# A list scheduler that ranks by latest start in four passes, in a fused Fourier and DeltaNet layer

## The chip, the cores and the metric

The kernel runs on one core of a Trainium2 chip. The metric is the device time of one execution in microseconds (us), the median over runs. The core's engines are TensorE (PE, with its weight loads shown apart as PEld), VectorE (DVE), ScalarE (ACT), GpSimd (POOL) and SyncE (SP). SP and ACT also issue the transfers; the trace shows these issues as SPq and ACTq.

## The reference

One layer over 1024 latent tokens and 256 context tokens, 1024 channels wide. The input is normalised and modulated, and projected by `w_in` into all branches. A Fourier branch takes a 2-D transform in 4 channel groups. A DeltaNet branch has 8 heads of 128 channels, two directions and chunks of 64 tokens, and needs a triangular solve in each chunk. The two branches are merged through gates, projected by `w_out`, added to the residual and normalised.

```python
def deltanet_branch(qkv, dn_gate, ...):
    qkv = jax.nn.silu(centred_depthwise_conv(qkv, conv_w))      # 3 taps along the tokens
    ...
    a_mat = where(strict, einsum('bhnid,bhnjd->bhnij', kb, k) * decay, 0) + eye(CHUNK)
    sol = triangular_solve(a_mat, rhs, lower=True, unit_diagonal=True)
    ...                                                         # scan over the chunks, both directions
    return o @ w_dn_out, s_f, s_b

def merge_branches(r_f, r_d, y_f, y_d, w_out):
    return (sigmoid(r_f) * y_f + sigmoid(r_d) * y_d) @ w_out

x_next = layer_norm(DEEPNORM_ALPHA * x + gate_x * out_x) * ln_g + ln_b
```

## The kernel before

**Products.** Everything is float32. The large products are made of three matmuls each (`mm3`, L622 to L624) on operands that are split into a high and a low part: a cast on ACT gives the high part (L602, `whi`, `zh`, `h`), a subtraction on POOL or DVE the low part (L603, `wlo`, `zl`, `l`). A weight block of 128 x 1024 is loaded into one of two `wraw` buffers (L677), split, and used in 48 matmuls of 512 columns that fill one "main" PSUM bank of 1024. There are two main banks and four smaller "s" banks. PE can begin the next block when the block before the last one has been read out of its main bank.

**Stages.** First come the modulation and norms, the Fourier branch and the context's keys and values. Then, for each of the 8 heads: the q, k and v blocks with their convolution on DVE (L1002 and L1003 read the main bank `main` and write `cv`, ACT L1006 and POOL L1008 and L1009 finish them), the decays, the inverse, and the scan over ten units of 128 tokens. The inverse (L1182 to L1246) is turned on DVE (L1182), solved in 30 row steps there (L1193 and L1196), turned back (L1198, L1201), and then put together on PE from 32 x 32 blocks: 80 small matmuls L1216 into one PSUM tile, a copy (ACT L1217), 80 small matmuls L1223 into a second tile `y2`, of which DVE (L1226, L1227) and ACT (L1229) read 32 partitions at a time.

**Tail.** `tail()` (from L1536) multiplies the DeltaNet output by `w_dn_out` in 8 blocks `nb`. Blocks 0 and 1 are started early and hold the two main banks. `merged(nb)` ends a block: DVE L1549 multiplies the loaded token gate `td` with the bank, which sets the bank free, POOL L1550 adds the Fourier part `af`, and the sum is split into `zh` and `zl`. `td` and `af` come by SP (L1645, names `t<-td`, `t<-af`) into four buffers `t` of the pool `z`, which takes the place of the heads' pool `dn`. Then `gated(kt)` loads a block of `w_out` and multiplies it with the gate `gx` (L1565): blocks 2, 3, 6 and 7 (`RAW`) go through the two `wraw` buffers, the others through four buffers `wo`. `source(i)` loads a tile of x into `t`, and ACT issues the position rows (L1589). At the end come the last product and the norm (L1621 to L1641).

**The order.** The kernel is recorded first. `schedule()` then walks through planned time, keeps a free time for each engine, PSUM bank and the port that DVE and POOL share (`locked`), and always places next the operation that can begin earliest, by rank where several can. `ranks()` gives the rank: program order in the head and the tail, the length of the path to the end in between. `touch()` finds which operations depend on which. The real waits come from the framework that builds the program out of the resulting order.

## Time and profile before

| | before |
|---|---|
| median of 3 runs | 1348.24 us (1345.63 to 1352.89) |
| profiled execution | 1346.62 us |
| its span in the trace | 1344.8 us |
| PE, PEld busy | 94%, 77% |
| DVE, ACT, POOL busy | 67%, 43%, 31% |
| chain that ended last | PE 73%, DVE 14%, ACT 5%, DMA 4%, issue 3% |

The span is what lies between the first and the last record; 1.8 us of the execution lie around it. Busy shares are over the whole span, the granted TensorE clock is given per stretch (1.00 is the higher of its levels). The chain is followed back from the last instruction, at each step to what released it.

### The profile page before, as it was taken

The numbers are of one execution on the slowest core, as the hardware profiler recorded it, in microseconds if no ns is written. First come the engines' busy times: TensorE is split into PE (matmuls) and PEld (weight loads), VectorE is DVE, ScalarE is ACT, GpSimd is POOL, SyncE is SP. The second block draws the span as 40 slices with busy tenths as digits, with TensorE's granted clock in tenths as the row PEclk, the third lists the DMA queues.
The fourth block names the chain that finished last, engine by engine and source line by source line (L and its number), as shares of the span: only waits on it lengthen the run. The fifth ranks groups of instructions, "written<-read, shape, count | busy, mean of one in ns | idle before, by whom it ended". The sixth has DMA issues, their size and how long they took to land.

```text
span 1344.8 us, 22842 instructions
## 1 busy us (share of the span) xinstructions
PE 1263.5 (94%) x8274; PEld 1036.9 (77%) x8274; DVE 904.9 (67%) x2680; ACT 584.2 (43%) x1611; POOL 414.2 (31%) x390
## 2 busy tenths in 40 slices
PE   7899999999799999999999999899999999699797
PEld 1478888888678888888788888788877888588686
DVE  6867554306686977978767869657968545445597
ACT  2653333324455366474474474545464544212000
POOL 3532233134552323322223323223412013236210
PEclk9999999999999999999999999999988999799899
DMA  9524333352313103113022131132121025743332
GB/s 318 187 68 138 118 112 102 118 180 83 83 33 90 53 27 100 48 44 115 32 79 79 33 87 55 34 99 59 32 88 48 33 94 175 252 160 112 102 116 78
DMA packets 51893, 129.92 MB, mean 97 GB/s; under 512 B 6242, under 2 KB 18915, under 8 KB 51780
## 3 DMA queue, kind: packets, MB, share of 16 engines
q1 hardware_dynamic: 44496, 114.02, 26.9%
q10 hardware_dynamic: 7284, 14.45, 3.1%
q8 instruction: 65, 1.06, 0.3%
q14 instruction: 48, 0.39, 0.1%
HBM read 105.29 MB, written 23.15 MB: 96 GB/s over the span
## 4 chain that ended last, share of the span: by engine, by line
PE 73%; DVE 14%; ACT 5%; DMA 4%; issue 3%; POOL 0%; ACTq 0%; SPq 0%; DVEq 0%; POOLq 0%
PE main L622 17%; PE main L623 16%; PE main L624 16%; PE s L1281 2%; PE s L1139 2%; PE s L1298 2%; PE s L1268 2%; DVE B L1193 2%; PE s L1310 2%; DVE X L1196 2%; PE s L1277 2%; PE s L1037 2%; PE s L622 1%; PE s L624 1%; PE s L623 1%
## 5 line engine op out<-in xcount | busy, mean ns | idle before, releaser
L622 PE MATMUL main<-h,whi 128*128 128x512 f32 x1024 | 412.6, 412 | 21.2 <-DVE t L1549 12.2
L624 PE MATMUL main<-h,wlo 128*128 128x512 f32 x1024 | 413.4, 413 | 0.4 <-POOL wlo L603 0.4
L623 PE MATMUL main<-l,whi 128*128 128x512 f32 x1024 | 412.2, 411 | 0.0
L603 POOL TENSOR_TENSOR wlo<-wraw,whi 128x512 fp32r<-128x512 f32 (+1 forms) x136 | 185.8, 1373 | 514.1 <-ACT whi L602 399.5
L622 PEld LDWEIGHTS main<-h,whi 128*128 128x128 f32 x1024 | 194.8, 191 | 55.4 <-issue 13.8
L623 PEld LDWEIGHTS main<-l,whi 128*128 128x128 f32 x1024 | 194.8, 191 | 31.0 <-issue 0.2
L624 PEld LDWEIGHTS main<-h,wlo 128*128 128x128 f32 x1024 | 194.0, 191 | 30.4 <-POOL wlo L603 0.9
L602 ACT CAST whi<-wraw 128x512 fp32r<-128x512 f32 (+1 forms) x176 | 102.7, 600 | 181.6 <-PE main L623 114.1
L1284 ACT ACTIVATE y<-s,ce 128x128 f32<-128x128 f32 x144 | 52.7, 366 | 138.0 <-PE s L1281 137.1
L1156 POOL TENSOR_TENSOR E<-E,mask 128x256 f32<-128x256 f32 x80 | 58.3, 750 | 175.4 <-DMA E<-gr 136.8
L1193 DVE TENSOR_TENSOR B<-X 128x110 f32<-128x110 f32 (+27 forms) x472 | 103.3, 258 | 0.0
L1196 DVE TENSOR_TENSOR X<-X,B 128x110 f32<-128x110 f32 (+27 forms) x472 | 101.7, 256 | 0.0
L1143 DVE SCALAR_TENSOR_TENSOR zp<-s,c,E 128x256 f32<-128x256 f32 (+1 forms) x160 | 65.4, 452 | 45.1 <-PE s L1139 34.1
L1302 DVE SCALAR_TENSOR_TENSOR S<-S,egl,s 128x128 f32<-128x128 f32 x128 | 43.5, 342 | 50.9 <-PE s L1298 50.1
L1270 DVE SCALAR_TENSOR_TENSOR R<-s,eG,vt 128x128 f32<-128x128 f32 x144 | 49.7, 345 | 33.6 <-PE s L1268 31.8
L1160 ACT ACTIVATE E<-E,nG 128x128 f32<-128x128 f32 x160 | 53.8, 398 | 31.8 <-POOL E L1156 31.7
L603 DVE TENSOR_TENSOR wlo<-wraw,whi 128x512 fp32r<-128x512 f32 (+1 forms) x40 | 31.2, 781 | 51.7 <-ACT whi L602 51.7
L1281 PEld LDWEIGHTS s<-R,zp 128*128 128x128 f32 x288 | 52.1, 190 | 14.9 <-ACT zp L1286 2.8
L1281 PE MATMUL s<-R,zp 128*128 128x128 f32 x288 | 56.5, 278 | 3.2 <-ACT zp L1286 1.6
L1298 PE MATMUL s<-y,ktok 128*128 128x128 f32 x288 | 56.8, 280 | 2.4 <-DVE acc L1293 1.5
L1298 PEld LDWEIGHTS s<-y,ktok 128*128 128x128 f32 x288 | 49.9, 192 | 11.1 <-DVE acc L1293 1.9
L1268 PEld LDWEIGHTS s<-S,kq 128*128 128x128 f32 x256 | 45.8, 190 | 14.0 <-DVE S L1302 2.8
(340 smaller groups left out, 2424.3 us busy)
## 6 DMA issues: line engine op xcount, KB each, us to landing
wraw<-in_win SPq DMA_DIRECT2D x72, 512.0 KB, 3.7
E<-gr SPq DMA_DIRECT2D x40, 256.0 KB, 4.9
wmod<-in_wm SPq DMA_DIRECT2D x32, 256.0 KB, 5.9
x<-in_x SPq DMA_DIRECT2D x8, 512.0 KB, 5.8
wgate<-in_wg SPq DMA_DIRECT2D x8, 512.0 KB, 3.7
yf<-yf ACTq DMA_DIRECT2D x8, 512.0 KB, 2.7
rfy<-yf SPq DMA_DIRECT2D x8, 512.0 KB, 4.8
af<-rfy SPq DMA_DIRECT2D x8, 512.0 KB, 3.8
```

The source lines that it names most:

```text
L602: self.nc.scalar.copy(out=hi, in_=x)
L603: (eng or self.nc.gpsimd).tensor_tensor(out=lo, in0=x, in1=hi.bitcast(F32), op=ALU.subtract)
L622: mm(ps, lhsT=lh, rhs=rh, start=first, stop=False)
L623: mm(ps, lhsT=lh, rhs=rl, start=False, stop=False)
L624: mm(ps, lhsT=ll, rhs=rh, start=False, stop=last)
L1143: v.scalar_tensor_tensor(out=o, in0=ps.rearrange("p (a i) -> p a i", a=W), scalar=G.c[:, d, u:u + 1], in1=e[:, d, i].unsqueeze(1).to_broad ...
L1156: nc.gpsimd.tensor_tensor(out=e[:, d], in0=e[:, d], in1=self.mask[:, d].unsqueeze(1).to_broadcast([P, 2, P]), op=ALU.add)
L1193: v.tensor_tensor(out=B, in0=X[:, c0::2, l:l + 1].to_broadcast([P, w, l]), in1=X[:, l:l + 1, :l].to_broadcast([P, w, l]), op=ALU.mult)
L1196: v.tensor_tensor(out=X[:, c0::2, :l], in0=X[:, c0::2, :l], in1=B, op=ALU.subtract)
L1268: mm(ps, lhsT=G.k(u), rhs=S[d], start=True, stop=True)
L1281: mm(ps, lhsT=zp[:, d, u], rhs=R[d], start=True, stop=True)
L1298: mm(ps, lhsT=G.ktok[:, u], rhs=y[d], start=True, stop=True)
```

## The change

The instructions are nearly the same (6380 on PE in both); what differs is mainly their order and which buffers some tiles lie in.

1. `schedule()` runs four passes. Each pass (`place()`) is the old walk; after it `latest()` goes backwards through the order found and gives each operation the latest planned start that doesn't lengthen the plan. The next pass ranks by that, in the head and the tail too. The pass with the shortest plan is kept.
2. `touch()` counts a PSUM tile as a whole when it looks for dependencies.
3. The shared port is given back in the plan when the operation leaves its engine, not when its result has landed.
4. A new pool `share` holds three tiles of the inverse: X and Y (tag `s0`) and C (tag `s1`). In the tail the token tiles rotate over `s0`, `s1` and two buffers `t`. The first two, block 0's `td` and `af`, no longer wait for `dn` to close.
5. Blocks 6 and 7 of `w_out` are loaded into the buffers of `whi` and `wlo`.
6. The last tile's norm no longer gives half of its columns to ACT and POOL: L1628, L1630 and L1631 go, and L1636 runs on both halves.

```diff
...
-RAW = (2, 3, 6, 7)
+RAW = {2: 'wraw', 3: 'wraw', 6: 'whi', 7: 'wlo'}
...
+PASSES = 4
...
-        bits, (p0, p1) = v.bits, v.p
+        bits, (p0, p1) = v.bits, (0, P) if b.psum else v.p
...
     def schedule(self):
+
         self.finish()
         self.ranks()
+        best = None
+        for _ in range(PASSES):
+            done = self.place()
+            if best is None or self.span < best[0]:
+                best = self.span, done, {b: b.slot for o in done for b in o.opens or ()}
+            self.latest(done)
+        self.span, done, slots = best
+        for b, k in slots.items():
+            b.slot = k
+        return done
+
+    def latest(self, done):
+
+        end = self.span
+        after, late = dict.fromkeys(ENGINES, end), {}
+        for o in reversed(done):
+            l = min(end - (o.end - o.start), after[o.eng] - o.occ)
+            for s in o.succ:
+                k = s.pred[o]
+                l = min(l, late[s] - (o.occ if k == 1 else o.end - o.start + hop(o, s)))
+            for s in o.follow:
+                l = min(l, late[s])
+            late[o] = l
+            if o.eng == "PE":
+                after["PE"] = l
+        for o in done:
+            o.rank = -late[o]
+
+    def place(self):
...
             if o.lock:
-                locked["POOL" if e == "DVE" else "DVE"] = o.end
+                locked["POOL" if e == "DVE" else "DVE"] = t + o.occ + (1 if e == "DVE" and t != locked[e] else -30)
...
-        X = dn.tile([P, 32, 32], F32, tag="X", name="X")
+        X = self.share.tile([P, 32, 32], F32, tag="s0", name="X")
...
-            branches = lambda nb: (self._load(sp, "t", self.td[nb], 4), self._load(sp, "t", self.af[nb], 4))
+            turn = itertools.cycle((("s0", self.share, 1), ("s1", self.share, 1), ("t", sp, 2), ("t", sp, 2)))
+
+            def token(src):
+
+                tag, pool, bufs = next(turn)
+                return self._load(pool, tag, src, bufs)
+
+            branches = lambda nb: (token(self.td[nb]), token(self.af[nb]))
...
-                w = self._load(*((self.wp, "wraw", a["wo"][kt], 2) if kt in RAW else (sp, "wo", a["wo"][kt], 4)))
+                w = self._load(*((self.wp, RAW[kt], a["wo"][kt], 2) if kt in RAW else (sp, "wo", a["wo"][kt], 4)))
...
-                x = self._load(sp, "t", a["x"][i], 4)
+                x = token(a["x"][i])
...
-                if last:
-                    nm = sp.tile([P, 1], F32, name="nm")
-                    v.tensor_scalar(out=nm, in0=mv[:, 0:1], scalar1=-1.0, scalar2=None, op0=ALU.mult)
-                    c = halves[0]
-                    act.activation(out=y[:, c], in_=y[:, c], func=AF.Identity, bias=nm)
-                    gp.tensor_tensor(out=y[:, c], in0=y[:, c], in1=lng[:, c], op=ALU.mult)
...
-                for c in halves[last:]:
+                for c in halves:
...
-            self.C = self.dn.tile([P, 32, 32], F32, name="C")
+            self.C = self.share.tile([P, 32, 32], F32, tag="s1", name="C")
...
```

The lines of the changed kernel have other numbers: L1033 and L1034 are L1002 and L1003 of before, L1213, L1224 and L1227 are L1182, L1193 and L1196, L1229 and L1232 are L1198 and L1201, L1254 is L1223, L1372 is L1341, L1587 is L1549, L633 and L634 are L602 and L603.

**The entry of the tail, DVE.** The rows begin with the last gate products of head 7 (`silu`); `wlo` are low parts of the weights of blocks 2 and 3. Before:

```order
L1341 SCALAR_TENSOR_TENSOR silu_11863<-s,cst,silu_11863 128x512 x2
L603 TENSOR_TENSOR l_12014<-silu_11863,h_12009 128x512
L603 TENSOR_TENSOR wlo<-wraw,whi 128x512 x2
L1549 SCALAR_TENSOR_TENSOR t<-t,main 128x1024 x2
L603 TENSOR_TENSOR zl_12116<-t,zh_12106 128x1024
```

Now, with `s_11405` the tile of block 0 in the pool `share`:

```order
L1372 SCALAR_TENSOR_TENSOR silu_11867<-s,cst,silu_11867 128x512 x2
L634 TENSOR_TENSOR l_12018<-silu_11867,h_12013 128x512
L1587 SCALAR_TENSOR_TENSOR s_11405<-s_11405,main 128x1024
L634 TENSOR_TENSOR wlo<-wraw,whi 128x512
L1587 SCALAR_TENSOR_TENSOR t<-t,main 128x1024
L634 TENSOR_TENSOR wlo<-wraw,whi 128x512
```

Block 0's L1587 stands ahead of both `wlo`, block 1's between them.

**The entry of the tail, ACT,** with the semaphores that each waits for (those that begin with DMAHW are of transfers). Before:

```order
L1560 DMA gx<-gx 128x1024 [waits DMAHW0_49,DVE_49,DMAHW7_49,PE_49,Pool_49]
L1577 DMA lng<-in_lng 128x1024
L1578 DMA lnb<-in_lnb 128x1024
L1580 DMA ec<-in_ec 128x512
L602 CAST whi<-wraw 128x512 [waits DMAHW0_49,PE_49]
L602 CAST whi<-wraw 128x512
L1589 DMA rows<-in_er 64x512 [waits DMAHW0_49]
L1589 DMA rows<-in_er 64x512 [waits DMAHW1_49]
L1589 DMA rows<-in_er 64x512 [waits DMAHW3_49]
L1589 DMA rows<-in_er 64x512 [waits DMAHW4_49]
L602 CAST whi<-wraw 128x512 [waits DMAHW6_49,PE_49]
```

Now:

```order
L1598 DMA gx<-gx 128x1024 [waits DMAHW1_49,DVE_49,DMAHW2_49,PE_49,Pool_49]
L1627 DMA rows<-in_er 64x512 x3
L633 CAST whi<-wraw 128x512 [waits DMAHW2_49,PE_49]
L633 CAST whi<-wraw 128x512
L1627 DMA rows<-in_er 64x512 [waits DMAHW1_49]
L1618 DMA ec<-in_ec 128x512 [waits DMAHW2_49]
L1616 DMA lnb<-in_lnb 128x1024 [waits DMAHW4_49]
L1615 DMA lng<-in_lng 128x1024 [waits DMAHW6_49]
L633 CAST whi<-wraw 128x512 [waits DMAHW0_49,PE_49]
```

Four issues that wait for earlier transfers stand ahead of block 3's `whi` in both; they are other ones.

**The 32 x 32 products of the last head's inverse, PE,** with waits. Before:

```order
L1310 MATMUL s<-zp 128x128 [waits Activation_49]
L1223 MATMUL s<-C,Y 32x32 [waits DVE_49]
L1223 MATMUL s<-Ct,Y 32x32
...
L1223 MATMUL s<-C,Y 32x32
L1223 MATMUL s<-Ct,Y 32x32 [waits Activation_49]
L1223 MATMUL s<-C,Y 32x32
```

Now:

```order
L1308 MATMUL s<-S_10542,kq 128x128 [waits Activation_49]
L1254 MATMUL s<-C,Y 32x32 [waits DVE_49]
L1254 MATMUL s<-C,Y 32x32
L1254 MATMUL s<-Ct,Y 32x32 x2
...
L1254 MATMUL s<-Ct,Y 32x32 x2
L1299 MATMUL s<-S_10546,kq 128x128 [waits DVE_49]
```

The second wait, in the middle of the run, is gone. Before, seven of the eight inverses have it; now none does.

**The first head's inverse, DVE,** from the turn of C into X on; `cv<-main` are the convolutions that read a main bank, 511 and 512 columns each. Before:

```order
L1182 STREAM_TRANSPOSE X<-C 128x1024
L1002 SCALAR_TENSOR_TENSOR cv<-main,cst,cv 128x511
L1002 SCALAR_TENSOR_TENSOR cv<-main,cst,cv 128x512
L1193 TENSOR_TENSOR B<-X 128x30
...
L1193 TENSOR_TENSOR B<-X 128x126
L1003 SCALAR_TENSOR_TENSOR cv<-main,cst,cv 128x512
L1003 SCALAR_TENSOR_TENSOR cv<-main,cst,cv 128x511
L1002 SCALAR_TENSOR_TENSOR cv<-main,cst,cv 128x511
L1002 SCALAR_TENSOR_TENSOR cv<-main,cst,cv 128x512
L1003 SCALAR_TENSOR_TENSOR cv<-main,cst,cv 128x512
L1003 SCALAR_TENSOR_TENSOR cv<-main,cst,cv 128x511
```

Now:

```order
L1213 STREAM_TRANSPOSE X<-C 128x1024
L1033 SCALAR_TENSOR_TENSOR cv<-main,cst,cv 128x511
L1033 SCALAR_TENSOR_TENSOR cv<-main,cst,cv 128x512
L1034 SCALAR_TENSOR_TENSOR cv<-main,cst,cv 128x512
L1034 SCALAR_TENSOR_TENSOR cv<-main,cst,cv 128x511
L1224 TENSOR_TENSOR B<-X 128x30
...
L1229 STREAM_TRANSPOSE C<-X 128x32x32
L1033 SCALAR_TENSOR_TENSOR cv<-main,cst,cv 128x511
L1232 STREAM_TRANSPOSE Ct<-C 128x640
L1033 SCALAR_TENSOR_TENSOR cv<-main,cst,cv 128x512
L1034 SCALAR_TENSOR_TENSOR cv<-main,cst,cv 128x512
L1034 SCALAR_TENSOR_TENSOR cv<-main,cst,cv 128x511
```

The first block's convolution is now done before the row steps, the second block's after them; before, both ended in the middle.

## Rows read from the trace of the kernel before

**Rows 1.** page, part 1: busy us, share of the span, instructions
```profile
PE 1263.5 (94%) x8274; PEld 1036.9 (77%) x8274; DVE 904.9 (67%) x2680; ACT 584.2 (43%) x1611; POOL 414.2 (31%) x390
```

**Rows 2.** windows: stretch, length, busy us (x) of PE PEld DVE ACT POOL, PEclk, DMA share, GB/s
```profile
0.00:350.00 350.00, 328.14 (x1670) 252.98 (x1671) 187.27 (x376) 140.35 (x289) 120.30 (x135) 1.00 0.42 139
350.00:408.00 58.00, 47.74 (x428) 38.05 (x427) 50.41 (x176) 28.16 (x75) 30.28 (x20) 0.91 0.21 56
408.00:1100.00 692.00, 672.74 (x5181) 567.40 (x5181) 521.73 (x1849) 368.43 (x1151) 193.03 (x192) 0.99 0.21 64
...
1157.00:1170.00 13.00, 0.85 (x3) 0.50 (x2) 4.14 (x4) 1.14 (x2) 2.31 (x3) 0.64 1.02 358
...
1245.00:1256.00 11.00, 3.60 (x10) 2.07 (x9) 9.21 (x9) 3.32 (x5) 3.83 (x4) 0.70 0.70 206
```

**Rows 3.** waits of PE, whole span: engine line <- releaser: us, times, longest
```profile
PE main L622 <- DVE t L1549: 12.2, 1, 12.2
PE main L622 <- ACT kq L1006: 8.1, 1, 8.1
PE main L622 <- ACT h L602: 7.0, 1, 7.0
...
PE s L1223 <- ACT zp L1229: 4.6, 4, 2.5
...
PE s L1223 <- DVE T L1226: 1.9, 3, 0.7
```

**Rows 4.** timeline 1150 to 1172: start, us, engine, line, operation [idle before <- releaser]
```profile
1152.01 1.22 DVE L603 TENSOR_TENSOR l<-silu,h 128x512 fp32r<-128x512 f32 x1 [0.69 <-ACT h L602]
...
1153.35 0.32 SPq L1645 DMA_DIRECT2D t<-td  x1
...
1157.93 7.63 ACTq L1589 DMA_DIRECT2D rows<-in_er  x4
...
1165.66 1.14 ACT L602 CAST whi<-wraw 128x512 fp32r<-128x512 f32 x2 [9.08 <-DMA t<-af]
...
1166.88 1.33 DVE L603 TENSOR_TENSOR wlo<-wraw,whi 128x512 fp32r<-128x512 f32 x1 [8.86 <-ACT whi L602]
1168.14 2.34 DVE L1549 SCALAR_TENSOR_TENSOR t<-t,main 128x1024 f32<-128x1024 f32 x2
```

**Rows 5.** chain that ended last, 1165 to 1180: start, us, what
```profile
1173.68 0.43 PE main L622
...
1174.52 0.23 PE main L624
```

**Rows 6.** DMA issues, 1150 to 1172: KB each, median us to landing
```profile
t<-td SPq DMA_DIRECT2D x3, 512.0 KB, 5.8
```

**Rows 7.** timeline 1242 to 1257
```profile
1242.62 2.02 SPq L1645 DMA_DIRECT2D wraw<-in_wo  x2
...
1250.57 2.35 DVE L1565 TENSOR_TENSOR wraw<-wraw,gx 128x1024 f32<-128x1024 f32 x2
1251.88 2.28 ACT L602 CAST h<-wraw 128x512 fp32r<-128x512 f32 x4 [2.48 <-DMA rows<-in_er]
...
1252.55 1.22 PE L622 MATMUL main<-h,zh 128*128 128x512 f32 x2 [7.05 <-ACT h L602]
```

**Rows 8.** timeline of DVE, 352 to 392
```profile
368.24 1.40 DVE L1003 SCALAR_TENSOR_TENSOR cv<-main,cst,cv 128x512 f32<-128x512 f32 x2
...
386.46 2.06 DVE L1198 STREAM_TRANSPOSE C<-X 128x1024 f32<-128x1024 f32 x1
```

**Rows 9.** timeline 1336 to 1345
```profile
1336.46 0.74 DVE L1636 SCALAR_TENSOR_TENSOR yr<-yr,mv,lng 128x512 f32<-128x512 f32 x1
...
1337.44 1.26 POOL L1631 TENSOR_TENSOR yr<-yr,lng 128x512 f32<-128x512 f32 x1 [31.31 <-ACT yr L1630]
1337.49 1.23 DVE L595 TENSOR_TENSOR fint<-finy 128x1 f32<-128x1 f32 x1
...
1339.14 0.16 DVE L595 TENSOR_TENSOR fint<-finy 128x1 f32<-128x1 f32 x1
```

More of the change, by code (lines that the diff above doesn't have):

```diff
@@ L1211, in inverse @@
         y1, y2 = self.s()[:, :32 * NU], self.s()[:, :32 * NU]
-        Y = dn.tile([P, 32, 32], F32, tag="X", name="Y")[:, :NU]
+        Y = self.share.tile([P, 32, 32], F32, tag="s0", name="Y")[:, :NU]
         pairs = ((0, 0, 1), (0, 2, 3), (1, 1, 0), (1, 3, 2))
@@ L1233, in inverse @@
             y1, y2 = self.s()[:, :64 * n], self.s()[:, :64 * n]
-            Y = dn.tile([P, 32, 32], F32, tag="X", name="Y")[:, :16].rearrange("p (u a) i -> p u (a i)", a=2)[:, :n]
+            Y = self.share.tile([P, 32, 32], F32, tag="s0", name="Y")[:, :16].rearrange("p (u a) i -> p u (a i)", a=2)[:, :n]
             for u in us:
@@ L1678, in run @@
             self.both = False
+        self.share = self.pool("share")
         with ExitStack() as es:
```

## The prediction

> **What bounds the kernel now.** I read the page's busy shares first: PE is busy for 94% of the span and PEld for 77%, the next engine, DVE, for 67% [rows 1]. PE is the bound, its instructions stay the same, and so an order can only give back the time in which PE stands still or runs at its lower clock. The second view is the table of stretches, which shows where that is [rows 2]. Up to 350 us PE stands for 350 - 328.1 = 21.9 us; from 350 to 408 us for 10.3 us; from 408 to 1100 us, through seven heads, for only 692 - 672.7 = 19.3 us; from 1157 to 1170 us for 12.15 us, nearly the whole stretch; from 1245 to 1256 us for 7.4 us. The third view is the list of PE's waits, which names the releasers [rows 3]: the three longest single waits are 12.2 us for L1549 (the entry of the tail), 8.1 us for L1006 (the first head's inverse) and 7.0 us for a high part `h` (the last product). Then there is a wait of 4.6 + 1.9 us in seven pieces before L1223. These four places are what I cost; the rest of the order I treat as one term.
>
> **Entry of the tail.** The reader follows one timeline [rows 4]. The pool `dn` closes with the DVE subtraction that begins at 1152.01 us and takes 1.22 us; only then, at 1153.35 us, SP can issue the first `t<-td`. On ACT four issues of `rows` stretch over 7.63 us from 1157.93 us on, although each such issue is short: they wait, one by one, for earlier transfers. Behind them stands the cast of block 3's `whi` at 1165.66 us, behind that on DVE its `wlo` at 1166.88 us, and behind that, in DVE's order, L1549 at 1168.14 us, which alone could have set the main bank free for block 2. So PE waits for a block that it doesn't need yet. In the new order block 0's L1587 stands ahead of both `wlo`, and its tile lies in `share` and was loaded well before `dn` closed. It needs only block 0's last matmul, which PE reaches some 15 matmuls before its work is used up; 15 x 0.23 us = 3.4 us [rows 5] against 1.2 us for L1587 (2.34 us for two, [rows 4]). Block 2 can then begin without a wait.
>
> What is late next is block 3. PE works 48 matmuls x 0.23 us = 11 us on block 2, from about 1157.4 to 1168.4 us. By then block 1's bank must be free (its `td` is issued first after the close; such a load landed in 5.8 us in the median [rows 6], so about 1160 us) and block 3's `whi` and `wlo` must be done. If ACT's cast ends as before, at 1165.66 + 1.14 = 1166.8 us, and DVE's subtraction at 1168.2 us, it just fits. Price: 12.15 us of idle time, and the matmuls after it, which run at the lower level of the clock: in the chain they are 0.43 us each up to 1173.68 us and 0.23 us from 1174.52 us on [rows 5], the stretch's mean granted clock is 0.64 [rows 2]. Twelve of them cost 12 x 0.20 = 2.4 us. I leave 1 us for what remains: 12.15 + 2.4 - 1.0 = **-13.5 us** (from -8.5, with 6 us left for block 3, to -14.5).
>
> **The last product.** `w_out` blocks 6 and 7 went through the `wraw` buffers; the two issues are at 1242.62 us, their multiplication L1565 at 1250.57 us, the cast at 1251.88 us, and PE goes on at 1252.55 us after 7.05 us [rows 7]. In the new order they go into buffers of `whi` and `wlo`, which come free as blocks 6 and 7 of the DeltaNet product use theirs up; SP issues them ahead of the x tiles, and DVE has multiplied both before the last L1587. Price: 7.4 us idle [rows 2], and ten matmuls that took 3.60 us instead of 10 x 0.23 = 2.3 us at a mean clock of 0.70, 1.3 us more. I leave 2 us, as `zh` of block 7 still stands behind an issue of `rows` on ACT: 7.4 + 1.3 - 2.0 = **-6.7 us** (from -4.7 to -8.7).
>
> **The 32 x 32 products.** Before, the plan took the four quadrants of the tile `y2` as independent, and the real waits are on the whole tile: PE stopped in the middle of L1223's run until a reader of the finished quadrants was done. Now all 80 come first and the readers after. Price: the 4.6 + 1.9 = **-6.5 us** of [rows 3]. Against it the readers begin later, at most by half a run in eight heads; I take the near end and keep 3.5 us as the far one.
>
> **The first head's inverse.** Before, PE waited 8.1 us, since the convolution that frees a main bank ran only at 368.24 us, in the middle of the row steps [rows 3, 8]. Now it runs before them, so this wait goes. But the second block's convolution stands behind the whole inverse, after the turn back, which began at 386.46 us before [rows 8]. PE has 48 matmuls, 11 us, for the 25 us from 361.5 us to there. Before, after the wait it had both blocks and worked on until the inverse was through. I count it thus: the new order has some 25 matmuls (5.7 us) less behind it when the small products begin, and they begin about 2.7 us earlier, as two of four convolution pairs no longer lie within the row steps (1.40 us for a pair [rows 8]). Net **+3 us** (from -5, if other work fills the hole, to +6).
>
> **The end.** L1636 costs 0.74 us once more. It takes the place of L1630 and L1631, beside which DVE's L595 took 1.23 us where the same operation takes 0.16 us [rows 9]; this 1.07 us and the small L1628 go: **-0.5 us** (from 0 to -0.6).
>
> **The rest of the order.** In seven heads 19.3 - 6.5 = 12.8 us of PE's idle time are left [rows 2, 3], in many small waits of the scan. I take a quarter of it, **-3 us**; it can't be more than -12.8, and a poorer order could add as much as half, +6. Up to 350 us only few places move; I take nothing, and a fifth of the 21.9 us, 4 us, to either side. The passes themselves cost nothing on the chip, since they run when the program is built.
>
> Sum: -13.5 - 6.7 - 6.5 + 3 - 0.5 - 3 = -27.2 us on the profiled 1346.62 us, which gives 1319.4 us; the median of the runs shown is 1.6 us above the profiled execution, which is less than the terms are sure to. **Forecast: 1319 us.**
>
> **Rivals.**
> *B, the wait at the tail's entry only moves.* For it speaks that the transfers were saturated there: 358 GB/s over 13 us, the engines' share 1.02 [rows 2], 4.7 MB; only two loads of 0.5 MB leave this stretch, and in the new order four ACT issues that wait for earlier transfers still stand ahead of block 3's `whi`. Against it speaks that these wait for transfers that were issued early, and that block 3 now has 11 us of cover. If `whi` comes 9 us later than before, PE waits that long after block 2, the term falls from -13.5 to -4.5, and the time is 1328; with 3 us more left at the last product 1331. I give it 1325 to 1338. The Trainium skill, "DMA: Bandwidth & Descriptors", section "Issuing engines are not separate DMA queues", says that transfers from different issuing engines run on the same 16 engines and interleave, so that another order of issues doesn't shorten a burst; by this alone the burst would last as long less the two loads moved out of it, and this rival is what follows. The trace agrees in that SP's and ACT's issues land slowly together.
>
> *C, slower: banks held behind the inverse in every head.* What the first head shows could happen in all: a convolution put off behind the row steps. From 368.24 to 386.46 us are 18.2 us [rows 8]; less the 11 us that PE has in the other bank, a head could lose 7.2 us. Seven heads undo the gain from 27.2 / 7 = 3.9 us a head on, and at 5.5 us the time is 1319 + 38.5 = 1358. Against it: in the other heads PE also has the previous head's scan, and in the new order their convolutions stand within the row steps.
>
> *D, more than forecast.* If half of the 12.8 us goes (3.4 us more), the first inverse gains 5 us instead of losing 3, and the first 350 us give 4, the time is 1319 - 15 = 1304.
>
> *E, nothing that can be told.* If the heads' order costs 6 us instead of giving 3, half of the tail's 20 us comes back in another place and L1223 gives 3.5 us, it is 1319 + 9 + 10 + 3 + the 3 us of the worst first inverse = 1344.
>
> **How the numbers follow.** The forecast (1308 to 1327) gets 0.60, B 0.18, D 0.10, C 0.06, E 0.06. Half a per cent, 6.7 us, is about what a measurement of this kernel can tell from no change (the three runs shown lie 0.5% apart), so faster is below 1341.5. A, B and D lie there, less a little of B's upper end: 0.87; same 0.07; slower 0.06. The range goes from 1305 to 1338: it holds the forecast, B and half of D, 0.83, and leaves out C, E and D's lower half.
>
> **What would show it.** In the changed kernel's list of waits, PE's wait for the bank at the tail's entry should be under 2 us, and block 2's matmuls should run 0.23 us apart from the first; a wait of 6 us or more some 11 us later is B. The stretch before the last product should have no wait over 2 us. L1254 should have no idle time before it but at the start of a run. Around 373 to 388 us there should be a wait of some 10 us or more on a main bank, in place of the one at 361.5 us. If waits of over 3 us on main banks appear in each head, C holds. What would make the forecast wrong most easily is the seven heads: nearly all their instructions stand in another order, and I price that by one quarter of a small idle time.

## The result and the profile after

| | before | changed |
|---|---|---|
| median | 1350.36 us (1345.63 to 1352.89, 4 runs) | 1314.14 us (1308.25 to 1315.54, 4 runs) |
| profiled execution | 1346.62 us | 1308.25 us |
| span in the trace | 1344.8 us | 1306.5 us |

The ratio is 0.9727 [0.9685 to 0.977], faster by 36 us in the median. The profiled execution of the changed kernel is the fastest of its four, 6 us below their median (mean granted clock 0.985, in the others 0.982 to 0.983), so sums made from its trace lie at the fast edge.

The page, part 1, of the changed kernel (the columns of [rows 1]):

```profile
PE 1252.5 (96%) x8274; PEld 1027.8 (79%) x8274; DVE 921.2 (71%) x2680; ACT 586.5 (45%) x1610; POOL 415.4 (32%) x389
```

PE did the same work (8274 matmul records in both traces; the 6380 given above counts PE's instructions in the program) in 1252.5 us instead of 1263.5 us [rows 1], and stood for 1306.5 - 1252.5 = 54.0 us instead of 1344.8 - 1263.5 = 81.3 us. So the 38.3 us by which the span is shorter are 27.3 us of standing and 11.0 us in which the same work ran faster. I had looked almost only for the first kind. A part of the 11.0 us may belong to this execution and its clock, not to the order; 5.7 us of it are found below, in the 640 small products.

The stretches of the changed kernel that answer to [rows 2], with the same columns. Its later parts lie earlier in time: 1140 to 1160 us holds the entry of the tail, 1210 to 1230 us the last product.

```profile
0.00:350.00 350.00, 330.02 (x1656) 253.52 (x1657) 184.73 (x375) 139.69 (x285) 121.83 (x133) 0.98 0.43 139
350.00:408.00 58.00, 46.12 (x385) 37.31 (x384) 50.88 (x170) 25.38 (x69) 26.31 (x21) 0.85 0.23 65
408.00:1080.00 672.00, 659.41 (x5179) 554.45 (x5178) 530.93 (x1840) 368.78 (x1139) 192.35 (x194) 1.00 0.23 66
...
1140.00:1160.00 20.00, 20.00 (x90) 16.57 (x89) 11.01 (x8) 4.53 (x7) 8.17 (x4) 1.00 0.95 347
...
1210.00:1230.00 20.00, 20.00 (x89) 16.43 (x88) 19.97 (x14) 2.19 (x3) 17.37 (x10) 1.00 0.20 66
```

In both stretches of the tail PE is busy for the whole 20.00 us at the higher level of the clock (granted 1.00); before, 12.15 us and 7.4 us of idle time stood there [rows 2]. The first inverse (350 to 408 us) stands for 11.9 us, 1.6 us more than before. The heads (408 to 1080 us) stand for 12.6 us; before, it was 19.3 us.

The list of PE's waits that answers to [rows 3]:

```profile
PE s L1068 <- DVE kq L1042: 8.6, 2, 7.3
PE main L877 <- DVE cs L814: 5.2, 1, 5.2
PE s L1312 <- DVE acc L1324: 3.6, 2, 3.1
PE s L1247 <- DVE Ct L1232: 2.7, 1, 2.7
...
PE main L653 <- ACT h L633: 1.3, 1, 1.3
```

All four places that were costed have left the head of the list. What leads it now is the first head's inverse in a new form (L1068, L1247), and no wait on a main bank in any head (L653 to L655) is longer than 1.3 us, so rival C did not occur.

**The entry of the tail.** First SP's issue of block 0's later tile (its `af` was issued at 1057.27 us), then ACT and DVE there, by the timeline of each engine (columns as in [rows 4]):

```profile
1070.24 0.32 SPq L1677 DMA_DIRECT2D s<-td  x1
```

```profile
1151.05 0.33 ACTq L1615 DMA_DIRECT2D lng<-in_lng  x1
1151.48 1.14 ACT L633 CAST whi<-wraw 128x512 fp32r<-128x512 f32 x2 [8.04 <-DMA wo<-in_wo]
```

```profile
1141.32 1.22 DVE L1587 SCALAR_TENSOR_TENSOR s<-s,main 128x1024 f32<-128x1024 f32 x1 [1.46 <-PE main L655]
1143.54 1.36 DVE L634 TENSOR_TENSOR wlo<-wraw,whi 128x512 fp32r<-128x512 f32 x1 [1.00 <-ACT whi L633]
1144.82 1.21 DVE L1587 SCALAR_TENSOR_TENSOR t<-t,main 128x1024 f32<-128x1024 f32 x1
1152.66 1.41 DVE L634 TENSOR_TENSOR wlo<-wraw,whi 128x512 fp32r<-128x512 f32 x1 [6.64 <-ACT whi L633]
```

Block 0's tiles were issued 71 us and more before DVE uses them. DVE's L1587 for block 0 begins 1.46 us after DVE came free, released by PE's last matmul; this is the wait that should remain, on DVE's side and not on PE's. Block 3's `whi` is still late: it stands behind issues on ACT that wait for transfers, and begins at 1151.48 us. It sets off DVE's `wlo`, which is done at 1154.1 us. PE is still busy with block 2 then and wants it only about 1155.5 us (an estimate: 48 matmuls, 10.9 us, before PE's last matmul of block 3, which sets off that block's L1587 at 1166.48 us). So the end of the burst that rival B speaks of is hidden behind block 2, with about 1.5 us to spare.

The burst itself is there as before: in the 32 us from about the close of the pool `dn` on, the transfers ran at 299 GB/s and a share of 0.82 (1139 to 1171 us), before at 304 GB/s and 0.84 (1153 to 1185 us). The Trainium skill, "DMA: Bandwidth & Descriptors", section "Issuing engines are not separate DMA queues", says that transfers issued by different engines run on the same 16 DMA engines and interleave; the trace agrees in that the other order of issues left these two figures as they were. What changed is what waits for the burst.

**The last product.** DVE's timeline:

```profile
1202.37 1.59 DVE L1603 TENSOR_TENSOR whi<-whi,gx 128x1024 f32<-128x1024 f32 x1 [2.03 <-DMA whi<-in_wo]
...
1206.12 2.32 DVE L1603 TENSOR_TENSOR wlo<-wlo,gx 128x1024 f32<-128x1024 f32 x1
...
1210.00 1.22 DVE L1587 SCALAR_TENSOR_TENSOR t<-t,main 128x1024 f32<-128x1024 f32 x1 [1.56 <-PE main L655]
```

As forecast, both multiplications lie ahead of the last L1587, and the wait of 7.0 us is gone.

**The small products.** All of L1223 before, and all of L1254 after, by windows of one line (columns: PE busy, PEld busy, PEclk, DMA share, GB/s):

```profile
0.00:1345.00 1345.00, 12.78 (x640) 11.09 (x640) 0.98 0.30 97
```

```profile
0.00:1306.00 1306.00, 7.09 (x640) 6.20 (x640) 0.99 0.31 99
```

Not only the idle time before these 640 matmuls went (6.5 us to 0.1 us); the matmuls themselves take 7.09 us instead of 12.78 us.

**The first inverse.** PE's timeline:

```profile
375.32 0.25 PE L1118 MATMUL s<-part,fold 128*32 128x8 f32 x8
382.85 1.11 PE L1068 MATMUL s<-cst,kq 128*128 128x128 f32 x4 [7.28 <-DVE kq L1042]
385.32 1.12 PE L1068 MATMUL s<-cst,kq 128*128 128x128 f32 x4 [1.35 <-DVE kq L1042]
...
389.55 0.27 PE L1247 MATMUL s<-Ct,zp 32*32 32x32 f32 x2 [2.68 <-DVE Ct L1232]
```

A hole of some 10 us was forecast between 373 and 388 us. It is there, 7.28 + 1.35 + 2.68 = 11.3 us. The instruction that stands first is L1068, which waits for DVE's `kq` (L1042, at 382.12 us among the row steps) and which PE's order puts ahead of the next main bank's matmuls; a wait on a bank was forecast.

**The end.** DVE's timeline:

```profile
1298.71 0.74 DVE L1668 SCALAR_TENSOR_TENSOR yr<-yr,mv,lng 128x512 f32<-128x512 f32 x1
...
1300.28 0.16 DVE L626 TENSOR_TENSOR fint<-finy 128x1 f32<-128x1 f32 x1
...
1302.03 1.54 DVE L1671 SCALAR_TENSOR_TENSOR yr<-yr,finy,lnb 128x512 f32<-128x512 f32 x3
```

From L1668 to L1671 it takes 1302.03 - 1298.71 = 3.3 us; before, it was 3.9 us, from 1336.46 us [rows 9] to L1639 at 1340.38 us. The small operation beside POOL's L1631 took 1.23 us [rows 9] and now, with POOL idle, 0.16 us.

### The profile page after: what moved, and what is told of

It is laid out like the page before. It is cut to its first block, busy times and chain, and to the rows that moved or that the text cites. A ratio compares the mean times of both kernels' runs of the same rounds, so it can differ in the third digit from the quotient of the medians.

```text
span 1306.5 us, 22833 instructions
## 1 busy us (share of the span) xinstructions
PE 1252.5 (96%) x8274; PEld 1027.8 (79%) x8274; DVE 921.2 (71%) x2680; ACT 586.5 (45%) x1610; POOL 415.4 (32%) x389
## 4 chain that ended last, share of the span: by engine, by line
PE 55%; DVE 5%; ACT 2%; issue 1%; DMA 1%; DVEq 0%; ACTq 0%; SPq 0%
PE main L653 12%; PE main L654 12%; PE main L655 12%; PE s L1312 2%; PE s L1329 2%; PE s L1299 2%; PE s L1170 2%; PE s L1308 2%; PE s L1068 1%; PE s L1341 1%; DVE B L1224 1%; PE s L654 1%; PE s L655 1%; PE s L653 1%; DVE X L1227 1%
## 5 line engine op out<-in xcount | busy, mean ns | idle before, releaser
L653 PE MATMUL main<-h,whi 128*128 128x512 f32 x1024 | 414.7, 412 | 1.9 <-ACT h L633 1.3
L655 PE MATMUL main<-h,wlo 128*128 128x512 f32 x1024 | 415.1, 412 | 0.0
L654 PE MATMUL main<-l,whi 128*128 128x512 f32 x1024 | 413.5, 410 | 0.0
L634 POOL TENSOR_TENSOR wlo<-wraw,whi 128x512 fp32r<-128x512 f32 (+1 forms) x136 | 182.6, 1349 | 541.7 <-ACT whi L633 418.6
L653 PEld LDWEIGHTS main<-h,whi 128*128 128x128 f32 x1024 | 193.9, 190 | 32.4 <-ACT h L633 1.5
L654 PEld LDWEIGHTS main<-l,whi 128*128 128x128 f32 x1024 | 194.2, 190 | 29.9 <-issue 0.2
L655 PEld LDWEIGHTS main<-h,wlo 128*128 128x128 f32 x1024 | 193.5, 190 | 30.6 <-issue 0.2
L633 ACT CAST whi<-wraw 128x512 fp32r<-128x512 f32 (+1 forms) x176 | 100.2, 599 | 187.6 <-PE main L654 107.0
L1224 DVE TENSOR_TENSOR B<-X 128x110 f32<-128x110 f32 (+27 forms) x472 | 109.9, 270 | 0.0
L1227 DVE TENSOR_TENSOR X<-X,B 128x110 f32<-128x110 f32 (+27 forms) x472 | 106.9, 264 | 0.0
L634 DVE TENSOR_TENSOR wlo<-wraw,whi 128x512 fp32r<-128x512 f32 (+1 forms) x40 | 40.1, 1002 | 71.0 <-ACT whi L633 71.0
L1329 PEld LDWEIGHTS s<-y,ktok 128*128 128x128 f32 x288 | 50.5, 190 | 11.9 <-DVE S L1333 2.2
L1033 DVE SCALAR_TENSOR_TENSOR cv<-main,cst,cv 128x511 f32<-128x511 f32 (+1 forms) x48 | 34.2, 742 | 34.5 <-ACT cv L1030 34.3
```

Of the source, the lines that this page charges most:

```text
L633: self.nc.scalar.copy(out=hi, in_=x)
L634: (eng or self.nc.gpsimd).tensor_tensor(out=lo, in0=x, in1=hi.bitcast(F32), op=ALU.subtract)
L653: mm(ps, lhsT=lh, rhs=rh, start=first, stop=False)
L654: mm(ps, lhsT=lh, rhs=rl, start=False, stop=False)
L655: mm(ps, lhsT=ll, rhs=rh, start=False, stop=last)
L1224: v.tensor_tensor(out=B, in0=X[:, c0::2, l:l + 1].to_broadcast([P, w, l]), in1=X[:, l:l + 1, :l].to_broadcast([P, w, l]), op=ALU.mult)
```

## The experiments

The theory is that of the prediction: each part of the change takes away the wait that lies at its place (the early tiles the one at the tail's entry, the buffers of `whi` and `wlo` the one at the last product, the whole PSUM tile that before L1254). The rival is that the order found by the passes does this by itself, and the parts beside it add little. Every kernel below computes the whole layer and was timed in three rounds against the kernel before (its median was 1350.4 us beside the first four, 1351.1 us beside the others). Edits are of the changed kernel unless said otherwise.

| run | median, us (range) | ratio to before |
|---|---|---|
| u_raw | 1313.91 (1310.33 to 1318.51) | 0.9734 [0.9697 to 0.977] |
| u_share | 1311.61 (1310.31 to 1312.98) | 0.9715 [0.9685 to 0.9745] |
| u_psum | 1326.99 (1324.66 to 1329.2) | 0.9828 [0.9796 to 0.9861] |
| u_pass | 1342.12 (1339.25 to 1345.47) | 0.9937 [0.9919 to 0.9955] |
| b_pass | 1360.07 (1358.09 to 1362.13) | 1.0074 [1.0045 to 1.0102] |
| b_tail | 1344.7 (1336.43 to 1346.82) | 0.9948 [0.9926 to 0.997] |
| x_pairs | 1315.12 (1312.24 to 1317.14) | 0.9745 [0.9717 to 0.9774] |
| x_bank | 1316.77 (1313.77 to 1319.62) | 0.9759 [0.9729 to 0.9789] |
| u_lock | 1336.44 (1333.93 to 1343.07) | 0.9896 [0.9865 to 0.9926] |
| m_pass | 1316.25 (1313.27 to 1319.77) | 0.9742 [0.9702 to 0.9783] |
| p2 | 1312.45 (1311.18 to 1314.77) | 0.9715 [0.9677 to 0.9753] |
| p8 | 1312.15 (1309.7 to 1313.99) | 0.9705 [0.966 to 0.9749] |

**u_raw: blocks 6 and 7 back in the `wraw` buffers.**

```diff
-RAW = {2: 'wraw', 3: 'wraw', 6: 'whi', 7: 'wlo'}
+RAW = dict.fromkeys((2, 3, 6, 7), 'wraw')
```

> The changed kernel, but blocks 6 and 7 of w_out go through the two wraw buffers again. Theory A (each part removes the wait at its own place): the wait before the last product comes back, 7 to 10 us with its matmuls at the lower clock, so 1322 to 1326 us; nothing moves before 1200 us. Rival B (the four passes find the gain, the buffers matter little): the passes put other work into the hole, at most 3 us come back.

No loss that can be told. A row of PE's waits, and DVE's timeline, of this kernel:

```profile
PE main L654 <- POOL l L634: 1.7, 1, 1.7
```

```profile
1213.59 1.22 DVE L1587 SCALAR_TENSOR_TENSOR t<-t,main 128x1024 f32<-128x1024 f32 x1 [2.63 <-PE main L655]
...
1218.14 4.55 DVE L1603 TENSOR_TENSOR wraw<-wraw,gx 128x1024 f32<-128x1024 f32 x2
```

The load is late again and both L1603 stand behind the last L1587, yet PE waits only 1.7 us: in this order PE has other work behind it until they are done. So the buffers are not needed for this term, as I had it, and the rival holds.

**u_share: X, Y and C back in `dn`, the token tiles on four buffers `t`.**

```diff
-        X = self.share.tile([P, 32, 32], F32, tag="s0", name="X")
+        X = dn.tile([P, 32, 32], F32, tag="X", name="X")
...
-            turn = itertools.cycle((("s0", self.share, 1), ("s1", self.share, 1), ("t", sp, 2), ("t", sp, 2)))
+            turn = itertools.cycle((("t", sp, 4),))
...
-            self.C = self.share.tile([P, 32, 32], F32, tag="s1", name="C")
+            self.C = self.dn.tile([P, 32, 32], F32, name="C")
```

> The changed kernel, but the inverse's X, Y and C lie in the pool dn again and all token tiles in four buffers t of the tail's pool. Theory A in its simple form (block 0's early load is what removed the wait at the tail's entry): 12 to 14 us come back, about 1327 us. Theory A2 (what removed it is that L1587 no longer stands behind block 3's wlo and whi; the early load is worth only the landing time of one td, some 5 us after the pool closes): 3 to 6 us come back, 1317 to 1320 us. Rival B (the passes): under 2 us.

No loss either. A row of PE's waits and DVE's timeline:

```profile
PE main L653 <- DVE t L1587: 1.7, 1, 1.7
```

```profile
1146.46 1.35 DVE L634 TENSOR_TENSOR wlo<-wraw,whi 128x512 fp32r<-128x512 f32 x1 [3.67 <-ACT whi L633]
1147.73 1.21 DVE L1587 SCALAR_TENSOR_TENSOR t<-t,main 128x1024 f32<-128x1024 f32 x1
1154.53 1.41 DVE L634 TENSOR_TENSOR wlo<-wraw,whi 128x512 fp32r<-128x512 f32 x1 [5.58 <-ACT whi L633]
```

Block 0's tile is late here, as before the change, but L1587 stands between the two `wlo`, no longer behind both [rows 4]. With this order the late tile costs PE 1.7 us instead of 12.2 us: what held PE was DVE's order, far more than the pool that closes late.

**m_pass: both edits together,** so that the passes and the two models of the plan are left, and the last tile's norm.

> The changed kernel with both of the tail's edits of buffers undone at once (inverse's tiles and token tiles as before, w_out 6 and 7 through wraw); passes, PSUM and port model and the shorter last norm stay. Theory B2 (with the passes the order alone covers the tail's waits): 1312 to 1320 us, with waits of under 3 us at both places. Rival A (each covered for the other, the tail has only one slack): one of the two waits comes back with 5 us or more, 1320 us or more.

The waits are 1.8 us (L1587) and 1.7 us (L654), and the interval overlaps that of the changed kernel. With the passes there, the two buffer edits are worth 2 us by the medians, which three rounds cannot tell from nothing.

**u_pass: one pass,** with everything else of the change.

```diff
-PASSES = 4
+PASSES = 1
```

> The changed kernel with one pass, so with the ranks of before, but the whole PSUM tiles, the port's model and the tiles as changed. Theory A: the tail keeps its gain, L1254 keeps its gain, the first 350 us are as before (3 us better than in the changed kernel), and the seven heads lose what the passes alone gave there, 3 to 6 us: within 4 us of the changed kernel. Rival B: the passes are the larger part of the gain, 15 us or more come back, over 1329 us.

28 us of the 36 us go. Rows of PE's waits, and DVE and ACT at the last product:

```profile
PE s L1299 <- DVE S L1333: 9.9, 3, 7.3
PE s L1068 <- DVE kq L1042: 8.6, 2, 8.1
PE main L653 <- ACT h L633: 6.1, 1, 6.1
```

```profile
1234.25 1.22 DVE L1587 SCALAR_TENSOR_TENSOR t<-t,main 128x1024 f32<-128x1024 f32 x1 [0.39 <-PE main L655]
...
1246.81 2.28 DVE L1603 TENSOR_TENSOR wlo<-wlo,gx 128x1024 f32<-128x1024 f32 x1
```

```profile
1249.17 1.14 ACT L633 CAST h<-wlo 128x512 fp32r<-128x512 f32 x2 [9.02 <-DVE wlo L1603]
```

This is u_raw's mirror image: the buffers of `whi` and `wlo` are used, and the wait at the last product is there with 6.1 us, since L1603 stands behind the splits that DVE does after the last L1587. The buffer without the order gains next to nothing at this place (6.1 us against 7.0 us before). In the whole PE stands for 1338.9 - 1262.4 = 76.5 us, 22.5 us more than in the changed kernel; by the table of stretches the heads hold 24.4 us of it (408 to 1100 us; 12.6 us in the changed kernel) and the first inverse 14.8 us.

**b_tail: before, with the early tiles, the buffers and the last norm,** but one pass and the old models; against the changed kernel:

```diff
-PASSES = 4
+PASSES = 1
...
-        bits, (p0, p1) = v.bits, (0, P) if b.psum else v.p
+        bits, (p0, p1) = v.bits, v.p
...
-                locked["POOL" if e == "DVE" else "DVE"] = t + o.occ + (1 if e == "DVE" and t != locked[e] else -30)
+                locked["POOL" if e == "DVE" else "DVE"] = o.end
```

> The kernel before with the tail's tiles in share, w_out blocks 6 and 7 in whi and wlo and the shorter last norm, but one pass with the ranks, the PSUM model and the port model of before. Theory A: both waits of the tail go, 20 to 24 us gained, about 1327 us. Theory B2: the entry's wait goes (the early td lets L1587 stand first), 14 us, but the last product keeps 6 us of wait since DVE multiplies block 7 late: 1333 to 1340 us.

Faster than before by 6 us only, less than either theory had. The rows of PE's waits that belong to the tail and to the first inverse, then DVE at the entry and ACT at the last product:

```profile
PE main L653 <- ACT kq L1037: 8.1, 1, 8.1
...
PE main L653 <- ACT zh L633: 5.1, 1, 5.1
...
PE main L653 <- ACT whi L633: 2.6, 1, 2.6
```

```profile
1162.24 1.22 DVE L1587 SCALAR_TENSOR_TENSOR s<-s,main 128x1024 f32<-128x1024 f32 x1 [2.01 <-PE main L655]
1170.78 1.34 DVE L634 TENSOR_TENSOR wlo<-wraw,whi 128x512 fp32r<-128x512 f32 x1 [7.32 <-ACT whi L633]
```

```profile
1250.49 1.14 ACT L633 CAST h<-wlo 128x512 fp32r<-128x512 f32 x2 [12.32 <-DVE wlo L1603]
1253.49 1.04 ACT L633 CAST zh<-t 128x1024 fp32r<-128x1024 f32 x1 [1.86 <-DVE l L634]
```

At the entry the wait falls from 12.2 us to 2.6 us without the passes: since block 0's tile is there early, the old ranks too put its L1587 ahead of block 3's `wlo`. So this run does not part the early load from the order that comes with it; no run here has an early tile with L1587 behind both `wlo`. What u_share and b_tail have in common is that order. At the last product 5.1 us are left: PE now waits for `zh`, which stands on ACT behind the cast of block 7, and that cast waits for L1603, which is late in DVE's order as in u_pass.

**b_pass: before, with the four passes alone** (`place()`, `latest()` and the loop; the old models and buffers).

```diff
+PASSES = 4
...
+        for _ in range(PASSES):
+            done = self.place()
...
+            self.latest(done)
```

> The kernel before with the four passes alone (tiles, buffers of w_out, PSUM model, port model and the last norm as before). Theory B2 (the passes' order removes the waits of the tail whatever the buffers are, and gives some 20 us in the heads when the PSUM tiles are modelled rightly): the waits at the tail's entry and before the last product fall under 3 us each, about 20 us gained, but L1223 keeps its second waits, so 1322 to 1332 us. Rival A (each part removes its own wait): the tail's two waits stay, within 6 us of before.

Slower than before by 9 us, which neither theory had. The page, part 1, and the stretch of the heads:

```profile
PE 1278.1 (94%) x8274; PEld 1048.8 (77%) x8274; DVE 922.7 (68%) x2680; ACT 587.5 (43%) x1611; POOL 412.9 (30%) x390
```

```profile
408.00:1100.00 692.00, 658.07 (x5218) 554.93 (x5218) 524.97 (x1833) 358.36 (x1103) 190.69 (x191) 0.97 0.20 59
```

The heads lie later here, but these 692 us hold nearly the same work as before (5218 matmuls, before 5181). In the tail it does what u_raw and u_share let one expect (the waits there are 3.4 and 3.7 us), and the first inverse keeps only 2.4 us of idle time. But in the heads PE stands for 692 - 658.07 = 33.9 us instead of 19.3 us [rows 2], at a mean clock of 0.97 instead of 0.99. In the whole span PE stands for 1358.3 - 1278.1 = 80.2 us, hardly less than before (81.3 us): the heads lose what the tail and the first inverse give back. The 13.5 us by which the span is longer are busy time, 14.6 us more for the same instructions; the lower clock (0.973 in the mean, before 0.980) makes up some 9 us of it by proportion, an estimate.

The plan that the passes keep is never longer than that of the first pass, but it is made with the old models of the port and of the PSUM tiles. That these models are what fails is shown by m_pass, which differs from b_pass in the two models and the last norm alone: 1316.25 us against 1360.07 us.

**u_psum: quadrants of a PSUM tile independent again in the plan.**

```diff
-        bits, (p0, p1) = v.bits, (0, P) if b.psum else v.p
+        bits, (p0, p1) = v.bits, v.p
```

> The changed kernel, but dependencies on PSUM tiles are found by partition again. Theory A: L1254 gets its second wait back, and with it two quadrants at a time: busy time from 7.1 to about 12.8 us and idle time from 0 to about 6 us, so 11 to 12 us more, about 1326 us. Rival B: only what the passes can't place differently comes back, 0 to 4 us.

13 us slower than the changed kernel, as the theory had it. All of L1254 in this kernel, by windows of the line:

```profile
0.00:1327.00 1327.00, 13.24 (x640) 11.55 (x640) 0.98 0.31 98
```

6.2 us are the matmuls' own (13.24 against 7.09 us), about 5 us their waits (2.5, 2.1 and 0.5 us in the list of PE's waits), which are back.

**x_pairs: the 80 products of L1254 two quadrants at a time,** all first before the readers. It asks whether the 5.7 us less of busy time comes from the waits or from which quadrants stand next to each other.

```diff
-        for u in range(NU):
-            for d, i, j in pairs:
+        for u, (d, i, j) in [(u, p) for two in (pairs[::3], pairs[1:3]) for u in range(NU) for p in two]:
```

> The changed kernel with L1254's 80 small matmuls in another order: first the 40 of quadrant pairs 0 and 3, then the 40 of the other two, with no wait between them (the recorded program's order; the passes may move others). If the half of L1223's loss that was busy time, not waiting, came from running two quadrants at a time in place of four: its busy time rises from 7.1 to 12 us or more, the kernel by about 5 us, 1317 to 1320 us. Rival (the busy time was stretched by the waits alone): 7.1 us as in the changed kernel, no change in time.

```profile
0.00:1313.00 1313.00, 10.88 (x640) 9.99 (x640) 0.98 0.31 99
```

That is the same view of this kernel, where the line is L1253: 10.88 us, less than the 12 us expected, with 0.1 us of idle time before the line. So 3.8 us of the 5.7 us come from four quadrants instead of two in turn; the other 1.9 us weren't separated. The whole time is 1 us longer, which can't be told from nothing; 5 us were expected.

**u_lock: the shared port held until the result has landed, as the plan had it before.**

```diff
-                locked["POOL" if e == "DVE" else "DVE"] = t + o.occ + (1 if e == "DVE" and t != locked[e] else -30)
+                locked["POOL" if e == "DVE" else "DVE"] = o.end
```

> The changed kernel with the port's model of before (the port is held until the DVE or POOL result has landed), four passes, whole PSUM tiles, new tiles. Theory M (the passes gain only as far as the model that they rank by is right, and the port's model is part of it): 5 to 15 us come back, 1319 to 1329 us, spread over the heads. Rival (the PSUM model is all that the passes needed): within 4 us of the changed kernel, 1310 to 1318 us.

22 us slower than the changed kernel, more than expected. Three stretches:

```profile
0.00:350.00 350.00, 325.41 (x1643) 249.22 (x1644) 187.20 (x371) 137.78 (x282) 120.10 (x131) 0.99 0.43 138
350.00:408.00 58.00, 41.45 (x192) 33.60 (x190) 47.82 (x152) 22.90 (x59) 31.40 (x20) 0.88 0.21 68
408.00:1080.00 672.00, 650.17 (x5113) 543.75 (x5114) 531.81 (x1829) 354.85 (x1095) 187.79 (x194) 0.99 0.20 62
```

PE stands 4.6 us longer up to 350 us, 4.7 us longer in the first inverse and 9.2 us longer in the heads, 18.5 us of the 25.9 us by which this span (1332.4 us) is longer. The longest single wait is a new one, 9.7 us before L1068 in the heads, for a result of DVE (`vT`, L1042). It is shown that the model makes the loss, and where most of it lies; by which of the many moved instructions it comes is not.

**x_bank: DVE's work on main banks ranked ahead of everything** from the second pass on, to take away the hole in the first inverse.

```diff
-            o.rank = -late[o]
+            o.rank = -late[o] + (30000 if o.eng == 'DVE' and any(b.psum and b.tag == 'main' for b in o.bufs) else 0)
```

> The changed kernel, but DVE's operations that read a main bank rank 30 us earlier than their latest start. In the first head the second convolution then stands in the middle of the row steps, not behind them. If the bank that is held causes the 7.3 us wait of PE there: that stretch's idle time falls from 11.9 to under 5 us and the kernel by 4 to 8 us, to about 1308 us. Rival (the row steps that this delays are as late as the bank): the wait moves to the small products, no gain, 1312 to 1320 us.

```profile
PE s L1247 <- ACT junk L1074: 2.6, 1, 2.6
PE s L1254 <- ACT Y L1248: 2.4, 1, 2.4
```

The hole goes, and its place is taken by these waits a little later; the stretch from 350 to 408 us still stands for 58 - 48.2 = 9.8 us, and the whole is no faster. So the bank that is held was not what bounds this stretch, and the 4 to 8 us expected did not come; that the inverse itself bounds it is argued, not shown.

**p2 and p8: two and eight passes.**

```diff
-PASSES = 4
+PASSES = 2
```

> The changed kernel with two passes. If the first backward pass brings most (ranks by latest start at all): 1312 to 1322 us. If the gain comes step by step: near the middle between one pass (1342 us) and four (1314 us), 1324 to 1332 us.

> The changed kernel with eight passes, of which the best plan is a later one than the fourth. Expected from both sides: a plan that is a thousandth shorter is far below what the plan gets wrong, so 1308 to 1320 us, no better than four passes beyond the interval. If the plan ranks orders truly, 1310 us or less.

Neither can be told from four. So the first backward pass already gives what can be measured, and no kernel here beats the changed one by more than the intervals.

## Why the prediction was right, and where its terms were not

The forecast was 1319 us, the median is 1314.14 us. The time lies 5 us off, the gain 9 us and more: 27.2 us were forecast, and it is 36.2 us between the medians and 38.3 us between the spans. That the time came nearer than the gain is luck of the base: the prediction subtracts from the profiled 1346.62 us, and the median beside the changed kernel was 1350.36 us. By the steps of the prediction, in the profiled executions:

| term | forecast, us | measured, us | from |
|---|---|---|---|
| entry of the tail | -13.5 | -14.5 | 12.15 idle and 2.4 of lower clock, both gone |
| last product | -6.7 | -8.7 | 7.4 and 1.3, both gone |
| 32 x 32 products | -6.5 | -12.2 | 6.5 idle to 0.1; busy 12.78 to 7.09 |
| first inverse | +3 | +1.6 | idle 10.3 to 11.9 |
| end | -0.5 | -0.6 | 3.9 to 3.3 |
| rest of the order | -3 | -2.1 | up to 350 us 21.9 to 20.0; heads 12.8 to 12.6 |
| sum | -27.2 | -36.5 | of 38.3 by which the span is shorter |

1.8 us have no place. The sum also meets the medians' difference, 36.2 us, but the profiled executions lie 3.7 and 5.9 us below the medians of their kernels, so an agreement to a microsecond is partly luck.

**The 32 x 32 products** are the step that was mis-sized most: I priced the idle time ahead of the line and took the line's busy time as fixed ("its instructions stay the same"). The order now has four quadrants in turn, where it had two, and the line takes 7.09 us instead of 12.78 us. That this shortens the run was not in any row of before, and the table of stretches hid it in the heads' busy time.

**The entry of the tail** was right in its size and in what is late next: block 3's weights came at 1151.48 us and were hidden. The prediction gave two reasons, the order of DVE and the early tile. The order is the one that counts: with it a late tile costs 1.7 us (u_share), and the early tile helped without the passes because it brought that order (b_tail).

**The last product** went the way that was forecast, both L1603 ahead of the last L1587, but the reason given, the buffers, is not the cause: without them u_raw waits 1.7 us, with them u_pass and b_tail still wait 6.1 and 5.1 us. What tells these runs apart is where L1603 stands among DVE's splits. That the size came right is partly luck.

**The rest of the order** was right by a sum of large parts that I did not see. The passes alone cost 9 us (b_pass), everything but the passes saves 8 us (u_pass), and together they save 36 us. This is not a sum of parts. With four passes, the two models are worth 43.8 us (from b_pass to m_pass); with one pass, 2.6 us (from b_tail to u_pass), less than the runs of either kernel spread. With the four passes, without the model of the port 22 us are lost, without that of the PSUM tiles 13 us. The prediction had set the models' price at nothing but L1223; its worst case for the heads, +6, was too small for what a wrong model does in b_pass (+14.6 us of standing in the heads, +14.6 us of busy time in the whole). That the pieces fit together was not something that the trace of before could show.

**The rivals.** B was priced by a `whi` that comes 9 us later than before; it came 11.6 us after the close of `dn` instead of 12.4 us, since the issue of `lng`, the last one ahead of it, waited only until 1151.05 us. Some 1.5 us later it would have begun to cost. C did not occur in any head. D and E lie outside the interval of the changed kernel.

## What to carry to other kernels

Here a better search in the scheduler paid only once its model was right: the search alone lost 9 us, the models alone gave less than could be told, and the two together most of the 36 us. So mend the model first, then search, and measure the two together. When PE waits for a late load, look at what stands between the load and the releaser in the releasing engine's order before giving the load another buffer: at both places here the releaser's place in that order decided, and the early buffer helped at one of them by letting the scheduler put the releaser first. Price busy time too when an order changes which small matmuls stand side by side.

## What the runs showed of the hardware

The 640 products of 32 x 32 took 7.09 us with four quadrants in turn, 10.88 us with two in turn and no waits between, 12.78 us with two in turn and a wait in the middle. One such instruction has the same mean duration in all of them, 0.19 us, so what differs is how many lie over one another: in the first inverse, the 80 products start between 402.2 and 402.9 us in the changed kernel and between 405.7 and 406.9 us in x_pairs. The Trainium skill, "TensorEngine Tiling (Array Packing)", section "Key Properties", says that different tiles can load weights and multiply in parallel; the trace agrees, as 640 x 0.19 us one after another would be 122 us.

An operation of DVE on 128 x 1 took 1.23 us beside a POOL operation, ending with it, and 0.16 us without one ([rows 9] and the end, above). The other way round there is one row: of the 16 operations of POOL on `kq` (L1039) in u_lock, one took 10.75 us, in the first inverse beside a run of DVE's row steps, where the median is 1.29 us. That the port between DVE and POOL makes both is argued, not shown; that the plan's model of it matters is shown by u_lock's 22 us.
